# A hybrid encoder layer on one core: the first gate pair's accumulator moves to another PSUM pool, pooled parts to another SBUF pool, A21's preparation beside the last gate pair, and a fourth early gate tile

## The chip, the cores and the metric

The kernel runs on one core of a Trainium2 chip. The metric is device time in microseconds (us), the median of several runs; less is better. The engines are named as the profile names them: PE is TensorE's matmul, PEld its weight load, DVE is VectorE, ACT is ScalarE, POOL is GpSimd, and SP is the engine whose queue issues most of the loads.

## The reference, cut to what matters

One layer, 1024 tokens by 1024 channels, all in fp32:

```python
n = rmsnorm(h, norm_mix_pre[l])
proj = n @ w_in[l]
p_in = proj[..., :o0]                       # pooling branch, 4 groups, windows 2/4/8/16
qkv = proj[..., o0:o1]...                   # stick-breaking attention, 8 heads
xq = proj[..., o1:o2]...                    # cross attention into 256 memory tokens
gates = jax.nn.sigmoid(proj[..., o2:])...   # 3 branches x 1024 channels
y_pool = pool_mixer(p_in, w_pool_mix[l], pool_scale[l]) @ w_pool_o[l]
y_sb = stick_breaking_attention(q, k, v) @ w_sb_o[l]
y_x = memory_cross_attention(xq, mem_n, w_mem_kv[l]) @ w_x_o[l]
merged = gates[:, :, 0] * y_pool + gates[:, :, 1] * y_sb + gates[:, :, 2] * y_x
h = h + rmsnorm(merged @ w_out[l], norm_mix_post[l])
...                                         # then a SwiGLU layer of width 2816
```

The change is in the part from the projection `n @ w_in` to the start of stick-breaking attention.

## The kernel before, in words

**Precision by parts.** Every fp32 operand is split into a high and a low part (`parts`: ACT casts the high one, line 256, and DVE subtracts it to get the low one, line 257). `mm3` then runs three matmuls for each block (lines 170 to 172: high by high, high by low, low by high), mostly 128x128 weights against 128x512 columns.

**The projection by quarters.** The normed, transposed activations are cut into two column halves `c` (0, 1) and two depth halves: "A11", "A12" belong to `c` = 0 and "A21", "A22" to `c` = 1. A *pair* of 128-row output tiles is made by seven products rather than eight (a Strassen-like scheme), from the combinations S1 to S4 of the A quarters and matching combinations of the weight quarters b11 to b22 (function `pairs`). In a pair, `opening` makes product 11 in a bank X and product 12 in a bank Y; S2, S3 and 22 then go onto X, and S1 and S4 use another bank Y. The sums are taken on DVE: line 447 in the opening, line 471 after S4, line 476 after S3. Line 476 reads X, so product 22, which goes onto X, waits for it. xq, q, k, v and the gates of branch 0, output tiles 0 to 5 (`PAIRED`), are made in this way. The value product `v` is written out by hand, with two banks in X and two in Y (lines 774 to 805), and `to_values` splits its results on ACT (line 361) and DVE (line 362) into `d` tiles that POOL writes to DRAM (line 768).

**Plain gate tiles.** The other gate tiles go by plain products (`gate_step`: 12 matmuls for a depth half, 24 for a tile and a column half). `early` makes some of them, for `c` = 0 alone, while DVE still prepares S1 to S4, and `EARLY` says how many. The rest stand in the list `later`; `fill` takes from it in equal shares between the units of stick-breaking attention. A21 is needed by plain gate tiles with `c` = 1 alone.

**Work beside the pairs.** Memory attention (`recall`) and the pooling branch (`pooled`) are in a list `background`, one step of which `aside` starts at three points of each pair. A step of `pooled` loads raw projections, sums them on DVE (lines 663 to 681), splits the mixture into parts `mh` and `ml`, runs three matmuls into bank `pv`, and splits the result again (lines 687, 688) into `d` tiles that POOL writes to DRAM (line 692).

**What sets the order.** Tiles come from pools with fixed numbers of buffers: PSUM `pa` 3 banks, `pz` 2, `pt` 2, `pv` 1; SBUF `d` 6, `r` 4, `b2` 8, `ws` 3. A tile waits until an earlier tile in its buffer has been read for the last time. A scheduler reorders instructions between engines when the program is built, so the order on each engine is not that of the code; loads on the SP queue keep the code's order.

Of the kernel before, what the change touches and what calls it, by code (L numbers as in the profile page):

```python
# [9 lines left out]
F32R = mybir.dt.float32r  # L10
# [17 lines left out]
SCALE = 0.125  # L28
LEAD = 8
HOLD = 3  # L30
EARLY = 3
PAIRED = 6
FILL_FIRST = 4
FILL_LAST = 8
# [5 lines left out]
def hybrid_block(  # L40
# [47 lines left out]
    def t_act():  # L88
        return act.tile([P, C], F32R, tag="act", name="act")
# [7 lines left out]
    def t_b2(dt=F32):  # L97
        return b2p.tile([P, C], dt, tag="b2", name="b2")
# [4 lines left out]
    def t_d(dt=F32):  # L103
        return dp.tile([P, C + 16], dt, tag="d", name="d")
# [4 lines left out]
    def t_r(dt=F32):  # L109
        return rp.tile([P, C + 16], dt, tag="r", name="r")  # L110
# [7 lines left out]
    def ps_a():  # L118
        return pa.tile([P, C], F32, tag="pa", name="pa")

    def ps_z():
        return pz.tile([P, C], F32, tag="pz", name="pz")
# [132 lines left out]
    def parts(src, hi, lo, eng=nc.vector):  # L255
        nc.scalar.copy(hi, src)  # L256
        eng.tensor_sub(lo, src, hi.bitcast(F32))  # L257
        return hi, lo

    def normed_x(k, c, t, kept=False):  # L260
        if not kept:
            load(t, x[k, c])
        nc.vector.scalar_tensor_tensor(t, t, gain(G_PRE, k), rbc[c], ALU.mult, ALU.mult)
        return t
# [168 lines left out]
    def quarters(src, m):  # L433

        raw = [[None, None], [None, None]]
        for h, i in ((0, 0), (1, 0), (0, 1), (1, 1)):
            raw[h][i] = t_b2()
            load(raw[h][i], src[m + i, h])
        return raw

    def opening(raw, sink, other=ps_a):
        (b11, b12), (b21, b22) = raw
        X, Y = ps_a(), other()
        product(X, w_parts(b11), "11", True)
        p1 = copied(X)
        product(Y, w_parts(b21), "12", True)
        nc.vector.tensor_add(p1, Y, p1)
        sink(0, 0, p1)
        return X

    def pairs(jobs, raws=None):

        raws = raws or [jobs[0][0]()]
        ahead = len(raws)

        opened = [opening(raws[j], jobs[j][1], (ps_a, ps_z)[j]) for j in range(ahead)]
        for j, (_, sink) in enumerate(jobs):
            (b11, b12), (b21, b22) = raws[j]
            if len(raws) == j + 1 < len(jobs):
                raws.append(jobs[j + 1][0]())  # L460
            X, Y = opened[j], ps_a()
            t = b11
            nc.vector.tensor_sub(t, b12, t)
            product(Y, w_parts(t), "S1", True)
            s5 = copied(Y)
            aside()
            nc.vector.tensor_sub(t, b22, t)
            product(X, w_parts(t), "S2")
            s2 = copied(X)
            product(Y, w_parts(b22), "S4")  # L470
            nc.vector.tensor_add(s2, Y, s2)
            sink(0, 1, s2)
            aside()
            nc.vector.tensor_sub(b12, b22, b12)
            product(X, w_parts(b12), "S3")
            nc.vector.tensor_add(s5, X, s5)
            sink(1, 1, s5)
            nc.vector.tensor_sub(b21, b21, t)
            if len(opened) == j + 1 < len(jobs):
                opened.append(opening(raws[j + 1], jobs[j + 1][1]))  # L480
            product(X, w_parts(b21), "22")
            sink(1, 0, X)
            aside()
# [7 lines left out]
    def to_gate(b, m):  # L491
        def sink(c, i, t):
            u = t_g() if c == 1 and i == 0 else t
            nc.scalar.activation(u, t, AF.Sigmoid)
            nc.gpsimd.dma_start(gated[b][m + i][c], u)
        return sink
# [20 lines left out]
    def early(m):  # L517
        for half in range(2):
            w = w_parts(first_gate[half]) if m == 0 else split(w_gate[KT + m, half])
            gate_step(KT + m, half, 0, w)  # L520
# [10 lines left out]
    early(1)  # L531
    xq_raws.append(quarters(w_q, 0))
    early(2)
    for q in range(HK):
        nc.vector.tensor_sub(sums[q], sums[q], xs[q])
        A["S2"][q] = parts(sums[q], t_a(F32R), t_a(F32R))
# [116 lines left out]
    def pooled(g, c):  # L653
        def step():
            win = 2 << g
            p_in = t_c()
            load(p_in[:, :C], raw_d[g][c])
            if c == 1:
                nc.vector.memset(p_in[:, C:], 0.0)
            else:  # L660
                load(p_in[:, C:], raw_d[g][1][:, :16])
                nc.vector.tensor_mul(p_in[:, C:], p_in[:, C:], rbc[1][:, :16])
            nc.vector.tensor_mul(p_in[:, :C], p_in[:, :C], rbc[c])
            s = p_in
            step_, width = 1, C + 16
            while step_ < win:
                width -= step_
                nxt = t_c()
                nc.vector.tensor_add(nxt[:, :width], s[:, :width], s[:, step_ : step_ + width])
                s = nxt  # L670
                step_ *= 2
            e = slice(C - win + 1, C)
            if c == 1:
                fix = small.tile([P, 16], F32, tag="fix", name="fix")
                nc.vector.tensor_mul(fix[:, : win - 1], s[:, e], rcnt[:, 17 - win :])
            mixed = s[:, :C]
            nc.vector.scalar_tensor_tensor(
                mixed, mixed, 1.0 / win, p_in[:, :C], ALU.mult, ALU.subtract
            )
            if c == 1:  # L680
                nc.vector.tensor_sub(mixed[:, e], fix[:, : win - 1], p_in[:, e])
            mh, ml = parts(mixed, t_d(F32R)[:, :C], t_d(F32R)[:, :C])
            pm = ps_v()
            gs = slice(g * P, (g + 1) * P)
            mm3(pm, mix_h[:, gs], mix_l[:, gs], mh, ml, True, True)
            hi, lo = t_d(F32R)[:, :C], t_d(F32R)[:, :C]
            nc.scalar.activation(hi, pm, AF.Copy, scale=gain(G_POOL, g))
            nc.vector.scalar_tensor_tensor(
                lo, pm, gain(G_POOL, g), hi.bitcast(F32), ALU.mult, ALU.subtract
            )  # L690
            for t, d in zip((hi, lo), ph_d[g][c]):
                nc.gpsimd.dma_start(d, t)
        return step
# [78 lines left out]
            nc.vector.tensor_sub(dst[j], x_[j], y_[j])  # L772

    (b11, b12), (b21, b22) = raw
    X, Y = [ps_a(), ps_a()], [ps_a(), ps_z()]
    v_product(Y, two(b21), "12", True)
    p2 = [copied(t) for t in Y]
    aside()
# [25 lines left out]
    v_product(X, two(b21), "22")  # L804
    to_values(1, 0, X)

    pairs([(lambda m=m: quarters(w_gate, m), to_gate(0, m)) for m in range(0, PAIRED, 2)])
    while background:
        aside()
    for q in range(HK):  # L810
        u = normed_x(q, 1, t_d()[:, :C])
        A["21"][q] = parts(u, t_act(), t_act())

# [6 lines left out]
        for half in range(2)  # L822
        for c in range(1 if b == 1 and m < EARLY else 0, NC)
    ]
    gate_units = list(dict.fromkeys((t, half) for t, half, _ in later))
    gate_w = {}

# [575 lines left out]
```

## Time and profile before

| | |
|---|---|
| median of 3 runs | 1493.74 us (1491.47 to 1495.3) |
| the profiled execution's own time | 1493.64 us |
| its span, first to last instruction | 1491.9 us |
| PE busy | 1445.1 us (97%) |
| DVE busy | 1030.6 us (69%) |
| ACT busy | 702.3 us (47%) |
| POOL busy | 332.5 us (22%) |

The span is what the trace covers; the execution's own time lies 1.74 us above it. Busy shares are averages over the whole span; what a stage waits for is read from the stage.

### The profile page before, as it was taken

What the parts mean: (1) busy time and instruction counts of PE and PEld (TensorE: products, weight loads), DVE (VectorE), ACT (ScalarE), POOL (GpSimd) and SP (SyncE); (2) the same over time, 40 slices, a digit from 0 to 9 for tenths busy, and PEclk for the clock granted to TensorE, in tenths of its full rate; (3) what the DMA queues carried; (4) which work ended last, traced back from release to release, by engine and by line L of the source; (5) the groups of instructions that cost most, each with busy time, mean ns of one, the idle gap of its engine ahead of it and who ended that gap; (6) DMA issues with size and microseconds to landing.
All of it is one profiled execution on the core that took longest, in us unless ns stands there. A gap on an engine that the chain in (4) does not pass through costs nothing.

```text
span 1491.9 us, 20986 instructions
## 1 busy us (share of the span) xinstructions
PE 1445.1 (97%) x6926; PEld 1199.2 (80%) x6926; DVE 1030.6 (69%) x1718; ACT 702.3 (47%) x1399; POOL 332.5 (22%) x612
## 2 busy tenths in 40 slices
PE   9989999889999899999999999999999999999997
PEld 7867889668888788878887777888888887788876
DVE  8897878785886878655514597765566666579476
ACT  8555655444654666521235673223333333444453
POOL 0211121222322433444445310000011111000011
PEclk9999999999999999999999999999999999999999
DMA  7734455565432441575455454444455555664445
GB/s 240 233 100 131 145 170 171 184 217 185 125 96 95 151 128 64 170 248 167 152 162 195 144 181 147 152 133 128 136 192 195 192 195 199 227 190 155 112 129 197
DMA packets 125070, 243.68 MB, mean 163 GB/s; under 512 B 16528, under 2 KB 20128, under 8 KB 124960
## 3 DMA queue, kind: packets, MB, share of 16 engines
q1 hardware_dynamic: 96800, 171.00, 37.3%
q0 software_dynamic: 27584, 70.29, 13.5%
q8 instruction: 54, 0.88, 0.3%
q10 hardware_dynamic: 576, 1.05, 0.2%
q14 instruction: 56, 0.46, 0.1%
HBM read 172.01 MB, written 69.73 MB: 162 GB/s over the span
## 4 chain that ended last, share of the span: by engine, by line
PE 81%; issue 7%; DVE 6%; DMA 2%; ACT 2%; POOL 2%; SPq 0%; POOLq 0%; DVEq 0%; ACTq 0%
PE pa L170 15%; PE pa L172 15%; PE pa L171 15%; PE pz L172 5%; PE pz L170 5%; PE pz L171 5%; PE pt L172 3%; PE pt L170 3%; PE pt L171 3%; PE pt L895 2%; PE pv L170 1%; PE pv L910 1%; PE pv L171 1%; PE pv L907 1%; PE pv L172 1%
## 5 line engine op out<-in xcount | busy, mean ns | idle before, releaser
L170 PE MATMUL pa<-act,wh 128*128 128x512 f32 (+1 forms) x584 | 230.8, 395 | 8.8 <-DVE d L362 3.5
L172 PE MATMUL pa<-act,wl 128*128 128x512 f32 (+1 forms) x584 | 228.5, 393 | 2.9 <-DVE wl L257 2.6
L171 PE MATMUL pa<-act,wh 128*128 128x512 f32 (+1 forms) x584 | 229.4, 393 | 0.0
L256 ACT CAST wh<-b 128x512 fp32r<-128x512 f32 x152 | 93.5, 621 | 151.3 <-PE pa L171 91.0
L170 PEld LDWEIGHTS pa<-act,wh 128*128 128x128 f32 x584 | 110.9, 190 | 33.0 <-issue 4.2
L172 PEld LDWEIGHTS pa<-act,wl 128*128 128x128 f32 x584 | 110.7, 189 | 26.1 <-DVE wl L257 3.8
L171 PEld LDWEIGHTS pa<-act,wh 128*128 128x128 f32 x584 | 110.9, 190 | 21.1 <-issue 0.2
L257 DVE TENSOR_TENSOR wl<-b,wh 128x512 fp32r<-128x512 f32 x152 | 103.6, 686 | 29.8 <-ACT wh L256 25.1
L164 ACT CAST wh<-ws 128x512 fp32r<-128x512 f32 (+1 forms) x119 | 72.7, 611 | 102.6 <-PE pa L171 34.2
L256 ACT CAST wh<-ws 128x512 fp32r<-128x512 f32 x80 | 49.9, 625 | 105.1 <-DVE ws L1167 39.9
L165 POOL TENSOR_TENSOR wl<-ws,wh 128x512 fp32r<-128x512 f32 x52 | 69.1, 1337 | 71.9 <-ACT wh L164 71.9
L256 ACT CAST d<-b 128x512 fp32r<-128x512 f32 x66 | 40.8, 622 | 91.6 <-PE pt L171 47.2
L257 DVE TENSOR_TENSOR d<-b,d 128x512 fp32r<-128x512 f32 x66 | 45.4, 691 | 52.4 <-ACT d L256 49.0
L170 PE MATMUL pa<-a,wh 128*128 128x512 f32 x192 | 75.9, 398 | 5.7 <-ACT wh L256 3.5
L165 DVE TENSOR_TENSOR wl<-ws,wh 128x512 fp32r<-128x512 f32 (+1 forms) x67 | 44.8, 673 | 48.9 <-ACT wh L164 29.7
L171 PE MATMUL pa<-b,wh 128*128 128x512 f32 x192 | 75.6, 395 | 0.0
L172 PE MATMUL pa<-a,wl 128*128 128x512 f32 x192 | 74.6, 392 | 0.0
L176 DVE TENSOR_TENSOR d<-pt,d 128x512 fp32r<-128x512 f32 (+1 forms) x96 | 60.7, 637 | 17.4 <-ACT d L175 16.9
L1133 POOL DMA_DIRECT2D ff<-c x44 | 23.7, 540 | 214.9 <-DVE c L1188 123.6
L175 ACT CAST d<-pt 128x512 fp32r<-128x512 f32 (+1 forms) x96 | 53.0, 559 | 37.3 <-PE pt L895 26.4
L876 DVE TENSOR_TENSOR_SCAN r<-a,zero 128x512 f32<-128x512 f32 (+1 forms) x64 | 54.4, 852 | 18.1 <-POOL a L864 18.0
L257 DVE TENSOR_TENSOR wl<-ws,wh 128x512 fp32r<-128x512 f32 x80 | 54.9, 689 | 16.6 <-ACT wh L256 14.2
(429 smaller groups left out, 3982.0 us busy)
## 6 DMA issues: line engine op xcount, KB each, us to landing
b<-in_w_ffn_in_dram SPq DMA_DIRECT2D x88, 256.0 KB, 2.7
d<-gt SPq DMA_DIRECT2D x48, 256.0 KB, 3.0
ws<-in_w_ffn_in_dram SPq DMA_DIRECT2D x44, 256.0 KB, 2.7
ff<-c POOLq DMA_DIRECT2D x44, 256.0 KB, 2.9
b<-ffS SPq DMA_DIRECT2D x44, 256.0 KB, 2.7
ws<-in_w_gate_dram SPq DMA_DIRECT2D x40, 256.0 KB, 3.8
gt<-g POOLq DMA_DIRECT2D x39, 256.0 KB, 3.0
b<-ff SPq DMA_DIRECT2D x33, 256.0 KB, 3.8
```

Source lines behind the costliest of these rows:

```text
L164: nc.scalar.copy(wh[:, :n], ws[:, :n])
L165: lo.tensor_sub(wl[:, :n], ws[:, :n], wh[:, :n].bitcast(F32))
L170: nc.tensor.matmul(ps, lh, rh, start=first, stop=False, skip_group_check=onto)
L171: nc.tensor.matmul(ps, lh, rl, start=False, stop=False, skip_group_check=onto)
L172: nc.tensor.matmul(ps, ll, rh, start=False, stop=last, skip_group_check=onto)
L175: nc.scalar.copy(hi, ps)
L176: nc.vector.tensor_sub(lo, ps, hi.bitcast(F32))
L256: nc.scalar.copy(hi, src)
L257: eng.tensor_sub(lo, src, hi.bitcast(F32))
L876: nc.vector.tensor_tensor_scan(ex[:, lo + 1 : C + 1], rest[:, lo:], zero.broadcast_to([P, C - lo]), start, ALU.mult, ALU.add,)
L895: nc.tensor.transpose(ptr[:, col + n * P : col + (n + 1) * P], att[i, j // 4][:, (j % 4) * P : (j % 4 + 1) * P], ident,)
L1133: nc.gpsimd.dma_start(ff_d[n][k], t)
```

## The change

`EARLY` goes from 3 to 4, with one more call of `early`. `pairs` takes a bank function for the first job's X (`first`), and the gate pairs pass `ps_z`; in the value product the two banks of Y are taken ahead of those of X. `pooled` takes `mh` and `ml` from pool `r` in place of `d`. A21's loads and normalization are called by `beside_last` at the start of the last gate pair, into `b2` tiles in place of `d` tiles, and its parts follow the pairs directly. The first four entries of `later` are sorted so that both depth halves of a tile with `c` = 0 come ahead of those with `c` = 1.

```diff
-EARLY = 3
+EARLY = 4
...
-    def opening(raw, sink, other=ps_a):
+    def opening(raw, sink, other=ps_a, bank=ps_a):
         (b11, b12), (b21, b22) = raw
-        X, Y = ps_a(), other()
+        X, Y = bank(), other()
...
-    def pairs(jobs, raws=None):
+    def pairs(jobs, raws=None, beside_last=None, first=ps_a):
...
-        opened = [opening(raws[j], jobs[j][1], (ps_a, ps_z)[j]) for j in range(ahead)]
+        opened = [
+            opening(raws[j], jobs[j][1], (ps_a, ps_z)[j], (first, ps_a)[j]) for j in range(ahead)
+        ]
...
-            if len(raws) == j + 1 < len(jobs):
+            if len(raws) == j + 1 and j + 1 < len(jobs):
                 raws.append(jobs[j + 1][0]())
+            elif beside_last is not None:
+                beside_last()
...
     early(2)
+    early(3)
...
-            mh, ml = parts(mixed, t_d(F32R)[:, :C], t_d(F32R)[:, :C])
+            mh, ml = parts(mixed, t_r(F32R)[:, :C], t_r(F32R)[:, :C])
...
-    X, Y = [ps_a(), ps_a()], [ps_a(), ps_z()]
+    Y, X = [ps_a(), ps_z()], [ps_a(), ps_a()]
...
-    pairs([(lambda m=m: quarters(w_gate, m), to_gate(0, m)) for m in range(0, PAIRED, 2)])
+    a21 = []
+    pairs(
+        [(lambda m=m: quarters(w_gate, m), to_gate(0, m)) for m in range(0, PAIRED, 2)],
+        beside_last=lambda: a21.extend(normed_x(q, 1, t_b2()) for q in range(HK)),
+        first=ps_z,
+    )
+    for q in range(HK):
+        A["21"][q] = parts(a21[q], t_act(), t_act())
     while background:
         aside()
-    for q in range(HK):
-        u = normed_x(q, 1, t_d()[:, :C])
-        A["21"][q] = parts(u, t_act(), t_act())
...
+    later[:2 * NC] = sorted(later[: 2 * NC], key=lambda n: (n[2], n[1]))
```

Three places of the built order show what moves. The change's line numbers are those of the changed file (a line such as 540 there is line 535 before).

The first is DVE while S2 to S4 are prepared, from the second depth half of the third early tile on (`wl_1101`; `wl` made at line 165 is the low part of a loaded weight tile). Before:

```order
L165 TENSOR_TENSOR wl_1101<-ws_1098,wh_1100 128x512
L535 TENSOR_TENSOR r_1012<-r_1012,act_230 128x512
L165 TENSOR_TENSOR wl_1262<-ws_1259,wh_1261 128x512
L257 TENSOR_TENSOR wl_1284<-b2_1023,wh_1283 128x512
L539 TENSOR_TENSOR act_292<-act_292,d_990 128x512
L257 TENSOR_TENSOR act_1180<-d_982,act_1179 128x512
L257 TENSOR_TENSOR wl_1302<-b2_1025,wh_1301 128x512
```

After:

```order
L165 TENSOR_TENSOR wl_1101<-ws_1098,wh_1100 128x512
L540 TENSOR_TENSOR r_1012<-r_1012,act_230 128x512
L165 TENSOR_TENSOR wl_1122<-ws_1119,wh_1121 128x512
L544 TENSOR_TENSOR act_292<-act_292,d_990 128x512
L257 TENSOR_TENSOR act_1220<-d_982,act_1219 128x512
L547 TENSOR_TENSOR d_979<-d_982,d_979 128x512
L257 TENSOR_TENSOR a_1166<-d_990,a_1165 128x512
L165 TENSOR_TENSOR wl_1141<-ws_1138,wh_1140 128x512
```

Two more weight splits (`wl_1122`, `wl_1141`, the fourth early tile) stand there, and the first pairs' own splits come later; the subtraction at line 467 that product S2 of the first pair waits for has two more DVE instructions ahead of it than before.

The second is PE at the end of the value product, where the first gate pair begins (`pa_3193` is its X and `pa_3194` its Y before; `pv_3101` is a step of `pooled`). Before:

```order
L171 MATMUL pa_3193<-a_1136,wh_3287 128x512
L172 MATMUL pa_3193<-a_1135,wl_3288 128x512
L170 MATMUL pv_3101<-d_3097,wh_1261 128x512
L171 MATMUL pv_3101<-d_3098,wh_1261 128x512
L172 MATMUL pv_3101<-d_3097,wl_1262 128x512
L170 MATMUL pa_3194<-act_613,wh_3213 128x512
L171 MATMUL pa_3194<-act_614,wh_3213 128x512
```

After (`pz_3233` is X and `pa_3234` Y, `pa_3280` the bank of product S1):

```order
L172 MATMUL pa_3234<-act_628,wl_3254 128x512
L170 MATMUL pv_3141<-r_3137,wh_1301 128x512
L171 MATMUL pv_3141<-r_3138,wh_1301 128x512
L172 MATMUL pv_3141<-r_3137,wl_1302 128x512
L170 MATMUL pz_3233<-a_1160,wh_3327 128x512
L171 MATMUL pz_3233<-a_1161,wh_3327 128x512
L172 MATMUL pz_3233<-a_1160,wl_3328 128x512
```

Before, product 12 (`pa_3194`) stands behind S2 and both steps of `pooled`; after, products 11 and 12 are done first, and S2 follows. The 12 matmuls of S2 are followed by S1 in `pa_3280`.

The third is DVE at the end of the last gate pair (`c_3739` and `c_3702` are the pair's sums before, `c_3791` and `c_3754` after; line 263 normalizes A21, and `act` tiles from line 257 are its low parts). Before:

```order
L471 TENSOR_TENSOR c_3739<-pa_3684,c_3739 128x512
L476 TENSOR_TENSOR c_3702<-pa_3598,c_3702 128x512
L263 SCALAR_TENSOR_TENSOR d_3800<-d_3800,g_sb_99,r_513 128x512
L263 SCALAR_TENSOR_TENSOR d_3807<-d_3807,g_sb_99,r_513 128x512
L263 SCALAR_TENSOR_TENSOR d_3814<-d_3814,g_sb_99,r_513 128x512
L257 TENSOR_TENSOR act_3804<-d_3800,act_3803 128x512
```

After:

```order
L263 SCALAR_TENSOR_TENSOR b2_3733<-b2_3733,g_sb_99,r_513 128x512
L257 TENSOR_TENSOR act_3857<-b2_3727,act_3856 128x512
L693 SCALAR_TENSOR_TENSOR d_3612<-pv_3607,g_sb_99,d_3611 128x512
L674 TENSOR_TENSOR c_3707<-c_3703 128x513
L257 TENSOR_TENSOR act_3861<-b2_3730,act_3860 128x512
L257 TENSOR_TENSOR act_3865<-b2_3733,act_3864 128x512
L682 SCALAR_TENSOR_TENSOR c_3707<-c_3707,c_3696 128x512
L257 TENSOR_TENSOR r_3711<-c_3707,r_3710 128x512
L475 TENSOR_TENSOR c_3791<-pa_3736,c_3791 128x512
L693 SCALAR_TENSOR_TENSOR d_3719<-pv_3714,g_sb_99,d_3718 128x512
L480 TENSOR_TENSOR c_3754<-pa_3638,c_3754 128x512
```

A21's eight DVE instructions moved from behind the last pair's two sums to ahead of them.

## Rows read from the trace of the kernel before

**Rows 1.** The page's first part: busy time, share of the span, instructions.

```profile
PE 1445.1 (97%) x6926; PEld 1199.2 (80%) x6926; DVE 1030.6 (69%) x1718; ACT 702.3 (47%) x1399; POOL 332.5 (22%) x612
```

**Rows 2.** Timeline of PE, 95 to 113 us: start, duration, line, operands, [idle before <-releaser].

```profile
98.11 0.50 PE L172 MATMUL pa<-act,wl 128*128 128x512 f32 x1 [1.01 <-DVE wl L257]
...
104.18 0.79 PE L170 MATMUL pa<-a,wh 128*128 128x512 f32 x1 [3.50 <-ACT wh L256]
...
112.54 0.36 PE L591 MATMUL pz<-c,r 128*128 128x256 f32 x1 [1.34 <-DMA r<-xq]
```

**Rows 3.** Windows: stretch, length, busy by engine (instructions), granted clock, DMA share, GB/s.

```profile
104.10:107.20 3.10, 3.02 (x8) 2.40 (x9) 2.99 (x5) 1.58 (x4) 0.53 (x1) 0.53 0.62 172
268.90:274.20 5.30, 5.30 (x13) 4.14 (x14) 0.85 (x2) 0.72 (x3) 1.59 (x3) 0.50 1.05 339
335.50:339.30 3.80, 3.80 (x12) 2.97 (x11) 2.24 (x4) 1.40 (x3) 0.00 (x0) 0.55 0.68 189
250.20:329.70 79.50, 71.50 (x317) 57.00 (x315) 62.46 (x115) 37.96 (x70) 21.33 (x40) 0.96 0.62 190
317.80:329.70 11.90, 9.97 (x42) 7.34 (x40) 7.34 (x14) 4.10 (x7) 2.67 (x5) 1.00 0.89 269
345.00:645.00 300.00, 293.56 (x1610) 249.62 (x1608) 224.26 (x343) 170.87 (x379) 102.84 (x266) 1.00 0.40 128
680.00:720.00 40.00, 40.00 (x175) 32.65 (x174) 21.07 (x28) 8.29 (x14) 17.85 (x14) 1.00 0.50 157
```

**Rows 4.** Timeline of DVE, 80 to 103 us.

```profile
80.51 0.69 DVE L165 TENSOR_TENSOR wl<-ws,wh 128x512 fp32r<-128x512 f32 x1
81.11 0.69 DVE L535 TENSOR_TENSOR r<-r,act 128x512 f32<-128x512 f32 x1
...
102.78 0.69 DVE L467 TENSOR_TENSOR b<-b,b 128x512 f32<-128x512 f32 x1
```

**Rows 5.** Timeline of PE, 263 to 275 us.

```profile
263.70 0.51 PE L170 MATMUL pv<-d,wh 128*128 128x512 f32 x1 [1.00 <-ACT d L256]
264.60 0.50 PE L171 MATMUL pv<-d,wh 128*128 128x512 f32 x1 [0.40 <-DVE d L257]
...
268.87 0.77 PE L170 MATMUL pa<-act,wh 128*128 128x512 f32 x1 [3.53 <-DVE d L362]
```

**Rows 6.** Timeline of ACT, 263 to 271 us.

```profile
266.06 0.69 ACT L687 ACTIVATE d<-pv,g_sb 128x512 fp32r<-128x512 f32 x1 [2.42 <-DMA v<-d]
```

**Rows 7.** Timeline of PE, 320 to 335 us.

```profile
320.54 0.50 PE L171 MATMUL pv<-d,wh 128*128 128x512 f32 x1 [0.75 <-DVE d L257]
...
325.96 0.50 PE L170 MATMUL pa<-b,wh 128*128 128x512 f32 x1 [0.44 <-ACT c L424]
...
329.75 0.50 PE L170 MATMUL pa<-act,wh 128*128 128x512 f32 x1 [0.78 <-DVE c L476]
...
334.77 0.50 PE L170 MATMUL pa<-act,wh 128*128 128x512 f32 x1 [1.97 <-ACT wh L256]
```

**Rows 8.** Timeline of DVE, 325 to 333 us.

```profile
325.47 0.75 DVE L688 SCALAR_TENSOR_TENSOR d<-pv,g_sb,d 128x512 fp32r<-128x512 f32 x1 [2.09 <-ACT d L687]
...
329.00 0.69 DVE L476 TENSOR_TENSOR c<-pa,c 128x512 f32<-128x512 f32 x1 [2.18 <-PE pa L172]
329.61 2.07 DVE L263 SCALAR_TENSOR_TENSOR d<-d,g_sb,r 128x512 f32<-128x512 f32 x3
331.59 1.29 DVE L257 TENSOR_TENSOR act<-d,act 128x512 fp32r<-128x512 f32 x2
```

**Rows 9.** Timeline of the SP queue's loads, 324 to 337 us.

```profile
324.50 3.11 SPq L116 DMA_DIRECT2D d<-in_x_dram  x4
327.67 9.33 SPq L116 DMA_DIRECT2D ws<-in_w_gate_dram  x5
```

**Rows 10.** Waits of PE, 345 to 640 us: us in total, times, longest.

```profile
PE pv L907 <- DVE b L376: 2.0, 4, 1.0
PE pa L172 <- DVE wl L257: 1.6, 1, 1.6
```

## The prediction

> **What bounds the kernel now.** I read the page's busy shares first: PE is busy 97% of the span and DVE 69% [rows 1], so the time is PE's own work plus the places where PE stands still. The page's shares can't say where these are. The timeline of PE shows them: three short stretches hold the largest waits, one near 104 us, one near 269 us, one around 330 us [rows 2, 5, 7]. The windows show what a wait costs on top: behind each of them the granted clock is 0.53, 0.50 and 0.55 over a few us, which is the lower of its two levels (1.2 instead of 2.4 GHz), though PE has matmuls without a break there [rows 3]. The pace to compare with is that of an undisturbed stretch, 175 matmuls in 40.00 us, 0.229 us each [rows 3].
>
> **Step A, the fourth early tile.** Before, product S2 of the first pair waits 3.50 us for ACT's cast of its weights (104.18 us) [rows 2]. That cast waits for a DVE subtraction, line 467, which starts at 102.78 us; DVE instructions of this size follow each other every 0.60 us there (80.51 to 81.11 us) [rows 4]. The fourth tile adds 24 matmuls on PE, 24 x 0.229 = 5.5 us, ahead of S2, taken from the later fill. It adds two weight loads, two casts and two subtractions. The loads and casts are hidden: ACT is busy 1.58 of 3.10 us in that stretch [rows 3]. The two subtractions stand ahead of line 467 and DVE has no gap, so S2 can start 2 x 0.60 = 1.2 us later than before. PE thus does 5.5 us of work for a delay of 1.2: 4.3 us. The slow clock behind the wait goes too, as the wait left is about the size of the one at 98.11 us (1.01 us), behind which the clock did not fall: 3.10 us for 8 matmuls against 1.83 gives 1.3 us. Of the 5.6 us I take 5.2, since line 447's sums, ahead of line 467 on DVE, now wait for a PE that comes later. Bounds: 3.9 (the clock falls anyway, and those tenths are lost) to 6.9 (also the DMA wait of 1.34 us at 112.54 us [rows 2] goes, because the first memory scores stand 14 matmuls later).
>
> **Step B, the banks.** At 268.87 us product 12 of the first gate pair waits 3.53 us for a `pa` bank that the value product's last splits (line 362) still read, and just before it two waits of 1.00 and 0.40 us are for the parts of a `pooled` step [rows 5]. Why the splits are late stands on ACT: line 687 waits 2.42 us until a value tile in its `d` buffer has been written to DRAM [rows 6]; line 361 is queued behind it, and DVE's 362 waits for that. The change acts on both ends: X lies in `pz` and Y in a bank read earlier, so products 11 and 12 need no splits; and with `mh` and `ml` out of pool `d`, each `pooled` step takes two of the six `d` buffers in place of four. Waits of 4.93 us, and 13 matmuls in 5.30 us that should take 2.97 (2.3 us), are at stake: 7.3 us. What is late next is S1, whose bank is now the one that the splits hold. By the order PE does 37 matmuls between the value product and that wait, in place of 28, 2.1 us more cover; with ACT's 2.42 us gone as well, 4.5 us against the wait of 3.53 and the 1.40 that no longer delay PE leave about 0.4; I put 1.0. Step B is worth 6.3 us, between 2.1 (the splits come no earlier) and 7.3.
>
> **Step C, A21 beside the last pair.** Around 330 us PE waits 0.75, 0.44, 0.78 and 1.97 us [rows 7], and 12 matmuls in 3.80 us should take 2.7 (1.1 us) [rows 3]: 5.0 us. The 1.97 is for the cast of a later gate tile's weights. Their loads stand behind A21's four loads in the SP queue, which went out at 324.50 us, and went out at 327.67 us [rows 9]. A21's loads now go into `b2` tiles that the second pair has left, ahead of the heads' q and k loads; these tiles are free well before, so I put the four loads (3.11 us of the queue) at nothing; if they were late, the first heads would be late by up to that. The price is on DVE: four normalizations (three in 2.07 us) and four subtractions (two in 1.29) [rows 8], 5.3 us, now ahead of the sums at lines 471 and 476, for which product 22 waits. From 317.8 to 329.7 us DVE is busy 7.34 us [rows 3]; with 5.3 more that is 12.7, while PE without its 0.75 and 0.44 us needs 10.7. So line 476 comes 2.0 us late where it was 0.78. Step C: 5.0 - 2.0 = 3.0 us, between -1.4 (all 5.3 on the path, and the slow clock again, 1.1) and 5.0.
> What the rows show is that DVE idles 2.09 and 2.18 us just there, waiting for others [rows 8], which takes in most of A21. The Trainium skill (PSUM — Partial Sum Buffer, "Engine vs sequencer instructions") says that VectorE's queue is strict first in, first out, which speaks against this move: whatever stands ahead of a sum delays it, needed or not. By that rule without the idle time, step C would be 5.0 - 5.3 = -0.3 us and the sum 1483.5 us.
>
> **Step D, given back.** From 345 to 645 us PE is busy 293.56 of 300 us [rows 3], so the 5.5 us taken from its fill come off the time, unless they covered a wait. The largest groups of waits there are 2.0 and 1.6 us [rows 10]. I give back a fifth, 1.1 us; bounds 5.5 back, and 3.6 gained if both groups go, since the shares of `fill` come out more even. Sorting `later` costs nothing: the same matmuls with the same weights.
>
> **The sum.** 5.2 + 6.3 + 3.0 - 1.1 = 13.4 us off the profiled execution's 1493.64 (span 1491.9 plus 1.74): **1480.2 us**. The median of the runs shown is 0.1 above that execution.
>
> **The rivals.**
> DVE takes the place of the banks. From 250.2 to 329.7 us DVE is busy 62.46 us; with A21 67.8. PE's 71.50 there hold 2.3 us of slow clock, so it needs 69.2 [rows 3]: DVE would have to be busy 98% of a stage without PE's waits. For it: that number. Against it: the loads it adds come at the end, where DVE idles. Step C falls to -1.4: 1484.6 us. Chance 0.17.
> The change doesn't do what it says at the bank: the value tiles' writes, not the pooled parts, hold the `d` buffers (line 687's releaser is a value tile), and the wait moves from product 12 to S1. Step B is 2.1: 1484.4 us. Chance 0.11.
> The fill was cover, so its 5.5 us are given back: 1484.6 us. For it: PE waits in the attention stage at all; against it: under 2.2% of that stretch. Chance 0.07.
> Slower: attention starves. The units with the shortest work get one half tile each, and if the waits in each of the four head pairs grow to what rows 10's groups hold now in all, and half as much again, 5.4 us, then 4 x 5.4 = 21.6 us come back: 1493.64 - 14.5 + 21.6 = 1500.7 us. It decides from 14.5 us of new waits on (19 for over 0.3%). Nothing in the profile asks for it. Chance 0.03.
>
> **How the numbers follow.** The forecast has 0.62, with a range of its own from 1476 to 1484. A measurement of this kernel can tell about 0.3%, 4.5 us, from no change. The upper end goes to two of the first three rivals together (13.4 - 4.4 - 4.2 = 4.8 us gained, 1488.8); the lower end takes in two thirds of what the upper bounds add (1.7 + 1.0 + 2.0 + 4.7 = 9.4 us). That gives 1473.5 to 1488.5. Faster: the forecast and the single rivals, but for 0.09 where two or three of them meet: 0.88; same 0.09; slower 0.03.
>
> **What the changed profile would show.** A: no wait over 1.5 us on PE before S2 of the first pair, and a clock of 1.0 around it. B: product 12 of the first gate pair without a wait, S1 with one under 1.5 us, no slow clock near 265 us; a wait of over 3 us at S1 would be the second rival. C: the gate weights' casts no longer waited for; a wait of some 2 us at line 476 (480 of the changed file) or at the casts queued behind line 471 on ACT; over 4 us there is the first rival. D: PE's waits in the attention stage within 2 us of before's. The prediction fails if a new wait of over 3 us with a slow clock behind it shows up elsewhere, since that alone costs over 5 us.

## The result, and the profile after

The changed kernel takes 1479.87 us (median), the kernel before on the same chip 1492.61 us; the ratio of their runs is 0.9904, 95% interval 0.9888 to 0.9919, so it is about 1% faster. The forecast was 1480.2 us. The profiled execution took 1478.91 us, 14.73 less than the one of before, with a span of 1477.2 us. One run of 4814.21 us is left out of the comparison.

The time is right, but its terms are not: steps A and B gained more than was forecast, step C gained nothing, and step D gave back more. The rest of the document is about that.

The page's first part, which answers to [rows 1]:

```profile
PE 1441.9 (98%) x6926; PEld 1198.7 (81%) x6926; DVE 1029.8 (70%) x1720; ACT 702.9 (48%) x1401; POOL 332.2 (22%) x612
```

PE does as many matmuls as before. The place to read is where it doesn't run. Three stages cover the change: up to the first matmul of the value product; from there through the three gate pairs, to 15 us after the last matmul of product S3; and the attention stage with the merge of the branches, up to the transposes of line 1068 (1078 of the changed file). First the windows of these three stages before, then the same after:

```profile
0.00:209.60 209.60, 197.86 (x979) 164.97 (x979) 168.82 (x344) 128.52 (x265) 38.02 (x87) 0.99 0.55 173
209.60:343.40 133.80, 123.49 (x691) 106.08 (x692) 104.69 (x199) 65.98 (x129) 26.85 (x52) 0.96 0.60 185
343.40:813.50 470.10, 462.35 (x2347) 387.86 (x2346) 301.62 (x449) 220.41 (x477) 192.16 (x342) 1.00 0.46 146
```

```profile
0.00:207.20 207.20, 202.46 (x1003) 169.44 (x1003) 169.85 (x346) 130.24 (x268) 38.56 (x88) 1.00 0.56 178
207.20:334.80 127.60, 122.91 (x712) 107.07 (x713) 103.11 (x199) 66.73 (x132) 27.37 (x53) 1.00 0.68 206
334.80:799.00 464.20, 455.13 (x2303) 381.99 (x2302) 301.44 (x449) 218.28 (x475) 190.76 (x340) 0.99 0.45 144
```

Length less PE's busy time: 11.7, 10.3 and 7.8 us before, 4.7, 4.7 and 9.1 after. The clock went up from 0.99 and 0.96 to 1.00 in the first two stages, and down to 0.99 in the third. The first two stages got better, the third worse.

Now place by place. PE's timeline from 95 to 114 us holds three waits, where [rows 2] had 1.01, 3.50 and 1.34 us (start, duration, line, operands, idle before and its releaser, as in all timelines here):

```profile
102.22 0.50 PE L172 MATMUL pa<-act,wl 128*128 128x512 f32 x1 [0.78 <-DVE wl L257]
...
105.28 0.50 PE L170 MATMUL pa<-a,wh 128*128 128x512 f32 x1 [0.47 <-ACT wh L256]
...
106.28 0.50 PE L170 MATMUL pa<-a,wh 128*128 128x512 f32 x1 [0.27 <-ACT wh L256]
```

S2 of the first pair starts at 105.28 us, 1.10 later than before, with 24 more matmuls done. The second place is the first gate pair. From 257 to 275 us, where [rows 5] had 1.00, 0.40 and 3.53, PE waits nowhere; the windows say it with 18.00 of 18.00 us. The ACT instruction of [rows 6] (line 692 now) waits 0.29 us for PE and for no transfer:

```profile
95.00:108.00 13.00, 11.48 (x48) 8.53 (x47) 13.00 (x22) 5.72 (x10) 2.13 (x4) 1.00 0.29 83
257.00:275.00 18.00, 18.00 (x81) 14.88 (x80) 14.83 (x31) 11.31 (x22) 5.86 (x11) 1.00 0.82 253
```

```profile
260.25 0.69 ACT L692 ACTIVATE d<-pv,g_sb 128x512 fp32r<-128x512 f32 x1 [0.29 <-PE pv L172]
```

The third is the last gate pair. PE's timeline from 295 to 335 us; the waits of [rows 7] are gone and others stand there:

```profile
302.66 0.50 PE L170 MATMUL pa<-act,wh 128*128 128x512 f32 x1 [1.03 <-ACT g L498]
...
311.75 0.50 PE L170 MATMUL pa<-a,wh 128*128 128x512 f32 x1 [2.34 <-ACT c L424]
...
316.20 0.50 PE L170 MATMUL pv<-r,wh 128*128 128x512 f32 x1 [1.00 <-ACT r L256]
```

The 2.34 us is for the copy (line 424) out of S1's bank, into which S4 goes next. ACT's timeline just there shows what the copy stood behind:

```profile
306.84 0.62 ACT L256 CAST act<-b 128x512 fp32r<-128x512 f32 x1 [0.17 <-DVE b L263]
309.32 0.62 ACT L256 CAST act<-b 128x512 fp32r<-128x512 f32 x1 [1.85 <-DVE b L263]
309.85 0.68 ACT L692 ACTIVATE d<-pv,g_sb 128x512 fp32r<-128x512 f32 x1
310.59 0.62 ACT L256 CAST act<-b 128x512 fp32r<-128x512 f32 x1
311.11 0.58 ACT L424 COPY c<-pa 128x512 f32<-128x512 f32 x1
```

The casts `act<-b` make A21's high parts. One of them waits 1.85 us for DVE's normalization, and the copy is queued behind it. The gate weights' loads now go out at 310.62 us on the SP queue (327.67 in [rows 9]) and nothing waits for them.

The fourth is the attention stage. PE's waits there, where [rows 10] had 2.0 and 1.6 us as the largest groups:

```profile
PE pv L917 <- DVE b L376: 3.0, 3, 1.2
PE pv L917 <- DVE d L176: 2.0, 2, 1.8
```

The longest, 1.85 us at 378.15 us, has the slow clock behind it, and so have the waits around 630 us, where the branches are merged:

```profile
378.00:386.00 8.00, 7.84 (x36) 6.93 (x37) 8.00 (x12) 5.18 (x11) 4.01 (x11) 0.79 0.34 118
629.00:640.00 11.00, 9.74 (x34) 7.52 (x35) 5.30 (x8) 3.69 (x6) 8.21 (x7) 0.84 0.96 326
```

### The profile page after: what moved, and what is told of

The parts are those of the page before. It is cut to its first block, busy times and chain, and to the rows that moved or that the text cites. A ratio compares the mean times of both kernels' runs of the same rounds, so it can differ in the third digit from the quotient of the medians.

```text
span 1477.2 us, 20998 instructions
## 1 busy us (share of the span) xinstructions
PE 1441.9 (98%) x6926; PEld 1198.7 (81%) x6926; DVE 1029.8 (70%) x1720; ACT 702.9 (48%) x1401; POOL 332.2 (22%) x612
## 4 chain that ended last, share of the span: by engine, by line
PE 89%; DVE 5%; ACT 2%; issue 2%; DMA 1%; POOL 0%; SPq 0%; DVEq 0%; POOLq 0%; ACTq 0%
PE pa L170 17%; PE pa L172 17%; PE pa L171 17%; PE pz L172 6%; PE pz L170 6%; PE pz L171 6%; PE pt L172 3%; PE pt L170 3%; PE pt L171 3%; PE pt L905 2%; PE pv L917 1%; PE pv L920 1%; PE pz L868 1%; PE pv L170 1%; PE pv L171 1%
## 5 line engine op out<-in xcount | busy, mean ns | idle before, releaser
L170 PE MATMUL pa<-act,wh 128*128 128x512 f32 (+1 forms) x576 | 225.4, 391 | 2.3 <-ACT wh L256 1.0
L172 PE MATMUL pa<-act,wl 128*128 128x512 f32 (+1 forms) x576 | 223.7, 390 | 1.7 <-DVE wl L257 1.2
L171 PE MATMUL pa<-act,wh 128*128 128x512 f32 (+1 forms) x576 | 224.4, 390 | 0.0
L170 PEld LDWEIGHTS pa<-act,wh 128*128 128x128 f32 x576 | 108.4, 188 | 24.5 <-ACT wh L256 1.9
L171 PEld LDWEIGHTS pa<-act,wh 128*128 128x128 f32 x576 | 108.4, 188 | 20.6 <-issue 0.2
L176 DVE TENSOR_TENSOR d<-pt,d 128x512 fp32r<-128x512 f32 (+1 forms) x96 | 60.3, 637 | 15.8 <-ACT d L175 15.1
L181 POOL TENSOR_TENSOR rc<-rv,mhalf 128x1 f32<-128x1 f32 (+2 forms) x15 | 14.7, 980 | 230.3 <-DVE rv L1306 198.6
```

Of the source, the lines that this page charges most:

```text
L170: nc.tensor.matmul(ps, lh, rh, start=first, stop=False, skip_group_check=onto)
L171: nc.tensor.matmul(ps, lh, rl, start=False, stop=False, skip_group_check=onto)
L172: nc.tensor.matmul(ps, ll, rh, start=False, stop=last, skip_group_check=onto)
L176: nc.vector.tensor_sub(lo, ps, hi.bitcast(F32))
```

## One account for all kernels

For each kernel below, the loss of a stage is the sum of PE's waits that the timeline lists in it and of the time lost to the lower clock (length times one less the granted clock, in windows of 5 us). For the kernel before and the change:

```
               to the value product   value product, gates   attention, merge
before         11.69 + 1.70 = 13.39   10.30 + 5.15 = 15.45   7.58 + 0.00 =  7.58
change          4.74 + 0.00 =  4.74    4.37 + 0.00 =  4.37   8.86 + 3.40 = 12.26
difference                   - 8.65                - 11.08               + 4.68
forecast        A            - 5.2     B and C     - 9.3     D           + 1.1
```

The three differences sum to -15.1 us, and the spans differ by 14.7. The account counts the lower clock also where PE stands still and loses nothing by it, 1.0 us in all for the kernel before. It is of one profiled execution for each kernel, and these don't all stand for the median: that of a21_later is the longest of its six (1486.31 us against a median of 1480.77), that of no_a21_last6 the longest of its four (1481.77 against 1477.25), those of low_on_pool and last6 the shortest (1478.8 against 1481.59, 1475.11 against 1476.97). What the account leaves over up to the transposes, which should be one number, lies between 773 and 778 us. So differences of 5 us or less between two kernels can't be rested on it alone; the single places can.

All twelve experiments, with the ratio to the kernel before on the same chip (its median was 1492.6 us beside the change and 1493.7 to 1495.4 beside the experiments); "early" is the number of early tiles, "A21" whether its preparation stands beside the last pair (moved) or behind it:

```
                early A21     ratio   95% interval      losses by stage
change           4    moved   0.9904  0.9888 - 0.9919    4.74   4.37  12.26
early_only       4    as was  0.9992  0.9981 - 1.0002    6.47  18.33  13.51   banks, r as before
no_early         3    moved   0.9884  0.9866 - 0.9903   14.52   5.98   4.30
no_bank          4    moved   0.9937  0.9919 - 0.9956    5.94  10.71   9.83
no_r             4    moved   0.9946  0.9931 - 0.9962    7.27  13.21   8.64
bank_r_only      3    as was  0.9933  0.9920 - 0.9946   13.56   4.39   8.17
no_a21           4    as was  0.9863  0.9844 - 0.9882    4.96   6.82   5.45
low_on_pool      4    moved   0.9917  0.9901 - 0.9934    4.59   7.58   8.56
casts_behind     4    moved   0.9913  0.9896 - 0.9930    5.80   3.99  12.38
a21_later        4    later   0.9918  0.9903 - 0.9934    6.38   7.16  16.41
no_sort          4    moved   0.9915  0.9899 - 0.9930    4.44   5.29  13.42
last6            4    moved   0.9892  0.9878 - 0.9906    4.85   5.47  11.54
no_a21_last6     4    as was  0.9890  0.9873 - 0.9906    6.97  11.37  10.54
```

## The experiments

**The early tile: early_only and no_early.** The kernel before with the fourth tile alone, and the change without it.

```diff
-EARLY = 3
+EARLY = 4
...
     early(2)
+    early(3)
```

> The kernel before with the fourth early gate tile and nothing else. Theory (the tile fills PE's 3.50 us wait before product S2 of the first pair, and what it takes from the later fill comes off the time): 5 to 8 us faster than before, no wait over 1 us before S2, the clock at 1.0 there. Rival (the fill was cover in the attention stage): within 2 us of before, with some 5 us of new waits between 345 and 640 us.

> The change without the fourth early tile. Theory (the parts add up): 6 to 8 us faster than before, that is 5 to 8 us slower than the change, with the 3.5 us wait and the slow clock near 104 us back. Rival (the early tile gives nothing that lasts): as fast as the change, 13 to 15 us faster than before.

Both rivals have the time right: alone the tile is worth nothing (1494.43 us, 0.9992), and the change without it is no slower (1479.75 us, 0.9884). Yet at its own place it does what was forecast, and more: the first stage loses 13.4 to 14.5 us in the three kernels with three tiles (before among them) and 4.4 to 7.3 us in the eleven with four. In early_only 6.9 us are gained there, and 2.9 and 5.9 are lost again in the two stages behind.

**The banks and the r tiles: no_bank, no_r and bank_r_only.** The change without `first=ps_z` and with X and Y in the order of before; the change with the pooled parts in `d` tiles; and the kernel before with these two edits and nothing else.

```diff
-    Y, X = [ps_a(), ps_z()], [ps_a(), ps_a()]
+    X, Y = [ps_a(), ps_a()], [ps_a(), ps_z()]
...
-        first=ps_z,
```

```diff
-            mh, ml = parts(mixed, t_r(F32R)[:, :C], t_r(F32R)[:, :C])
+            mh, ml = parts(mixed, t_d(F32R)[:, :C], t_d(F32R)[:, :C])
```

> The change with the first gate pair's X in pool pa again and the value product's banks in the old order. Theory (both the bank and the d buffers made the 3.5 us wait): product 12 of the first gate pair waits again, 1 to 3.5 us; 3 to 7 us slower than the change. Rival (freeing d buffers alone is enough): within 1 us of the change, no such wait.

> The change with the pooled parts in pool d again. Theory (the value product's last splits are late because d buffers are short): the wait moves to product S1 of the first gate pair, 1 to 4 us, 2 to 6 us slower than the change. Rival (the bank alone is enough): no wait at S1, within 1 us of the change.

> The kernel before with step B alone: X of the first gate pair in a pz bank, the value product's banks swapped, the pooled parts in r tiles. Theory 1, the parts add: the early tile is worth nothing, A21 beside the last pair costs 6 us, so step B alone must be worth nearly 20 us, about 1474. Theory 2, the parts do not add, and what A21's move costs is lost in the attention stage, whose order the scheduler makes anew for each kernel: step B alone is worth what the trace shows at its own places, the 4.93 us of waits and the slow clock behind them in the first gate pair, and the wait of 0.75 us in the last, some 8 us, less or more by what the attention stage happens to lose: 1482 to 1489, with the early stage's waits (1.01, 3.50, 1.34 us) still there and product 12 and S1 of the first gate pair without a wait.

Without the bank (1486.26 us) product 12 of the first gate pair waits for the value splits again, in PE's timeline from 255 to 275 us, with the clock at 0.77 behind it:

```profile
263.96 0.77 PE L170 MATMUL pa<-act,wh 128*128 128x512 f32 x1 [2.50 <-DVE d L362]
```

```profile
263.90:271.00 7.10, 7.04 (x24) 5.75 (x25) 3.27 (x6) 3.29 (x5) 1.60 (x3) 0.77 0.79 256
```

That is 4.2 of the 6.3 us that its second stage loses more than the change's. Most of the rest is in the last pair, where the wait for line 424 is 2.95 us and the slow clock stands behind it.

Without the r tiles (1487.54 us) the wait moves to S1, as the second rival had it, and a larger one appears in the last pair, for a cast of pooled parts:

```profile
272.62 0.47 PE L170 MATMUL pa<-act,wh 128*128 128x512 f32 x1 [1.99 <-DVE d L362]
...
317.68 0.49 PE L170 MATMUL pv<-d,wh 128*128 128x512 f32 x1 [4.87 <-ACT d L256]
```

At the first of these places ACT's line 361 waits 2.78 us until a value tile has been written to DRAM:

```profile
271.64 0.37 ACT L361 CAST d<-pa 128x256 fp32r<-128x256 f32 x1 [2.78 <-DMA v<-d]
```

At the second, DVE makes the last piece of the mixture (line 686) at 316.77 us, and the cast starts 0.07 us after its end. In this kernel's order A21's four normalizations and three of its subtractions stand ahead of that piece on DVE, from 309.21 us on, and DVE has no gap there. So this wait points to DVE's queue; that a `d` buffer is missing is not shown:

```profile
316.77 0.17 DVE L686 TENSOR_TENSOR c<-fix,c 128x15 f32<-128x15 f32 x1
317.01 0.62 ACT L256 CAST d<-c 128x512 fp32r<-128x512 f32 x1 [2.45 <-issue]
```

So at the first gate pair it takes both: the bank takes the splits off PE's path, and the r tiles let them run. Both by themselves (1483.57 us, 0.9933) give 10 us, and the trace of bank_r_only puts all of it into the second stage (15.45 to 4.39 us). Its first stage loses as much as before, and the third differs by 0.6. The theory that the parts simply add asked for 1474 and falls; the other, 1482 to 1489, holds.

**A21: no_a21, low_on_pool, casts_behind and a21_later.** A21 made behind the pairs again; its subtractions on POOL; its casts kept behind the pair's copies on ACT; and A21 made still later, behind two half tiles of `later`.

```diff
-        beside_last=lambda: a21.extend(normed_x(q, 1, t_b2()) for q in range(HK)),
...
-    for q in range(HK):
-        A["21"][q] = parts(a21[q], t_act(), t_act())
     while background:
         aside()
+    for q in range(HK):
+        u = normed_x(q, 1, t_d()[:, :C])
+        A["21"][q] = parts(u, t_act(), t_act())
```

```diff
-        A["21"][q] = parts(a21[q], t_act(), t_act())
+        A["21"][q] = parts(a21[q], t_act(), t_act(), nc.gpsimd)
```

```diff
-        nc.scalar.copy(t, ps)
+        tc.keep_in_program_order(nc.scalar.copy(t, ps))
...
-        A["21"][q] = parts(a21[q], t_act(), t_act())
+        hi, lo = t_act(), t_act()
+        tc.keep_in_program_order(nc.scalar.copy(hi, a21[q]))
+        nc.vector.tensor_sub(lo, a21[q], hi.bitcast(F32))
+        A["21"][q] = hi, lo
```

a21_later takes both A21 blocks of the first of these diffs out and puts the one with `t_d` here:

```diff
-    fill(FILL_FIRST)
+    fill(2)
+    for q in range(HK):
+        u = normed_x(q, 1, t_d()[:, :C])
+        A["21"][q] = parts(u, t_act(), t_act())
+    fill(FILL_FIRST - 2)
```

> The change with A21 made behind the gate pairs in d tiles again, loads included. Theory (A21 beside the last pair removes about as much as it brings: 1.97 us and a slow clock against waits of 2.34 and 1.00 us near 312 and 316 us): within 2 us of the change; the wait of 2.34 us gone, one of 1 to 2 us for a gate weight's cast back. Rival (the move is worth the 3.0 us of the forecast or more): 3 us or more slower than the change.

> The change with A21's four low parts subtracted on POOL instead of DVE. Theory (the 2.34 us wait near 312 us is ACT's queue: the copy of S1's result stands behind casts of A21 that wait for DVE's normalizations, and DVE is full there): two subtractions fewer ahead of the third normalization bring the copy 1.2 us earlier, so the wait falls to 1.0 to 1.4 us, and the time by 1 to 2 us. Rival (the copy is late by its own place): the wait stays at 2.3 us, the time as the change's.

> The change with A21's four casts kept behind the last pair's two bank copies on ACT. Theory (as above, ACT's queue order makes the wait): the 2.34 us wait is gone, the time falls by 1.5 to 3 us unless the first use of A21's parts then waits. Rival (PE waits for DVE in any order, since DVE is full): a wait of the same size, 2 us or more, moves to the last pair's sums, the time stays.

> The change with A21 made behind the first two half tiles of later, so that its loads stand behind those of the gate weights and its DVE work behind the last pair's sums. Without beside_last (A21 directly behind the pairs), DVE took A21's normalizations ahead of the sum that product 22 waits for, and stood 1.98 us for A21's load from DRAM, with that sum queued behind it: 3.61 us of PE's wait and 1.65 us of slow clock. Theory 1: the queue is the cause; with the sum ahead, that wait is at most 0.8 us (as in the kernel before) and the clock stays, some 4 us less than that kernel's 0.9863: about 1468 to 1470. Theory 2: A21 is then late for the first gate tile with c = 1, and PE waits there for ACT's casts or DVE's subtractions, 3 us or more, with the slow clock: 1472 to 1476.

no_a21 has the lowest time of all: 1472.59 us, 0.9863, faster than the change (the intervals don't meet), which neither its theory nor its rival had. At the place itself it is not better. Its PE timeline near 320 us has one wait of 3.61 us with the slow clock behind it, and DVE's shows why:

```profile
320.61 0.79 PE L170 MATMUL pa<-act,wh 128*128 128x512 f32 x1 [3.61 <-DVE c L480]
```

```profile
316.81 1.43 DVE L263 SCALAR_TENSOR_TENSOR d<-d,g_sb,r 128x512 f32<-128x512 f32 x2 [1.98 <-DMA d<-in_x_dram]
318.60 0.75 DVE L263 SCALAR_TENSOR_TENSOR d<-d,g_sb,r 128x512 f32<-128x512 f32 x1 [0.36 <-DMA d<-in_x_dram]
319.27 0.69 DVE L257 TENSOR_TENSOR act<-d,act 128x512 fp32r<-128x512 f32 x1
319.87 0.68 DVE L480 TENSOR_TENSOR c<-pa,c 128x512 f32<-128x512 f32 x1
```

The sum at line 480, for which product 22 waits, could run when PE ends S3 near 317 us. It runs at 319.87 us, because A21's normalizations stand ahead of it and wait for their own load. The Trainium skill (PSUM — Partial Sum Buffer, "Engine vs sequencer instructions") calls the queues of ScalarE and VectorE strict first in, first out; the trace agrees, on DVE here and on ACT with the 1.85 us of the change. In the prediction this rule was set against DVE's idle time and taken for covered; both traces show PE waiting behind such a queue, 2.34 us with A21 beside the pair and 3.61 behind it. By that rule without the idle time the prediction had put step C at -0.3 us, which comes nearer to what its stage shows than the 3.0 us that it took.

casts_behind takes A21's casts from ahead of the copy. The wait for the copy falls from 2.34 to 1.25 us, so the casts cost 1.09 of it, and two small waits (0.49 and 0.79 us) come up behind it. What is left stands behind a split of `pooled` (line 692), which itself waits for PE; the copy follows it at 310.71 us:

```profile
310.12 0.69 ACT L692 ACTIVATE d<-pv,g_sb 128x512 fp32r<-128x512 f32 x1 [2.77 <-PE pv L172]
```

The time stays (1480.54 us), where the theory asked for 1.5 to 3 us less. low_on_pool leaves the wait for the copy (2.16 us, where its theory asked for 1.4 at most), and a subtraction takes 1.3 to 1.7 us on POOL; 1481.59 us. a21_later, with the sum ahead of A21 on DVE, has no wait for line 480 any more, so the queue was the cause of the 3.61 us; but A21 is now late itself, as the second theory had it (the wait is shorter than its 3 us). Its PE timeline, in the first gate tile with `c` = 1:

```profile
331.44 0.50 PE L171 MATMUL pa<-act,wh 128*128 128x512 f32 x1 [2.02 <-DVE act L257]
```

Its second stage is no better than that of no_a21 (7.16 against 6.82 us). The kernel takes 1480.77 us, above the ranges of both theories (1468 to 1476); in its profiled execution, 5.5 us longer than that, the third stage loses 16.41 us against 5.45.

**What the attention stage loses: no_sort, last6 and no_a21_last6.** The change without the sorting of `later`; with two more half tiles (a depth half of a plain gate tile each) in the attention stage (54, as before the change, in place of 52); and no_a21 with these two.

```diff
-    later[:2 * NC] = sorted(later[: 2 * NC], key=lambda n: (n[2], n[1]))
```

```diff
-FILL_LAST = 8
+FILL_LAST = 6
```

> The change without the sorting of the first four later entries. Theory (sorting costs and brings nothing): within 1.5 us of the change. Rival (it hides A21's parts): a new wait of 1 us or more for A21's parts behind the last gate pair, 2 us or more slower.

> The change with FILL_LAST 6 in place of 8, so that 54 half tiles stand in the attention stage, as before the change, and not 52; 6 are left for the end. Theory 1, the fill was cover: with the two back the attention and the stage behind it lose about what they lost before (7.6 us of waits and slow clock) in place of 13.5, so about 1474. Theory 2, the amount says nothing and the waits come from the order that the scheduler makes: the waits are at other places than in the change and their sum can go either way, 1475 to 1484; in that case a kernel with 54 can lose as much as the change does.

> The change with A21 made behind the pairs as before (the fastest kernel so far, 0.9863) and 54 half tiles in the attention stage in place of 52. Theory 1, the attention stage's loss follows the order that the scheduler builds and nothing that the edit does: the order of TensorE's instructions there differs from that of each kernel run so far, so the waits stand at new places and their sum with the slow clock lies anywhere between 4.3 and 16.4 us, the ends seen so far (5.45 us without the two half tiles): 1471 to 1483. Theory 2, more fill covers more: 5.45 us or less, 1472 or less. In both the stages ahead of the attention lose what they lose without the two half tiles, about 12 us.

Sorting is worth nothing that can be measured (1481.07 us). last6 is 1476.97 us with an interval that meets the change's, and its third stage still loses 11.54 us (the 13.5 us that its expectation gives the change are 12.26 in the account). no_a21_last6 is 1477.25 us where no_a21 without the two half tiles is 1472.59; the intervals just overlap. In its profiled execution, 4.5 us longer than its median, the third stage lost more (10.54 against 5.45), and so did the two ahead (18.3 us, where 12 were expected). So the amount of fill alone doesn't set the loss: with 52 half tiles the stage lost 5.45 to 16.41 us, with 54 it lost 4.30 to 11.54.

What the waits follow is the order that the scheduler builds. Compared by source line and tile names, PE's instructions in this stage stand in the same order in the change and in no_bank, and differ in 2 places between low_on_pool and no_r, while the change and low_on_pool differ in more than 50. And the waits go with it. First the change, then no_bank, which is some 7 us later by then:

```profile
378.15 0.39 PE L917 MATMUL pv<-d,a 128*128 128x256 f32 x1 [1.85 <-DVE d L176]
...
538.52 0.39 PE L917 MATMUL pv<-d,a 128*128 128x256 f32 x1 [1.23 <-DVE b L376]
...
545.18 0.39 PE L917 MATMUL pv<-d,a 128*128 128x256 f32 x1 [1.17 <-DVE b L376]
```

```profile
385.14 0.39 PE L916 MATMUL pv<-d,a 128*128 128x256 f32 x1 [1.85 <-DVE d L176]
...
545.38 0.38 PE L916 MATMUL pv<-d,a 128*128 128x256 f32 x1 [1.23 <-DVE b L376]
...
552.05 0.38 PE L916 MATMUL pv<-d,a 128*128 128x256 f32 x1 [1.16 <-DVE b L376]
```

Then low_on_pool and no_r:

```profile
379.00 0.50 PE L867 MATMUL pz<-c 128*128 128x512 f32 x1 [1.13 <-ACT b L871]
...
384.38 0.51 PE L172 MATMUL pa<-act,wl 128*128 128x512 f32 x1 [0.76 <-DVE wl L257]
...
549.59 0.50 PE L172 MATMUL pa<-act,wl 128*128 128x512 f32 x1 [0.91 <-DVE wl L257]
```

```profile
385.73 0.50 PE L867 MATMUL pz<-c 128*128 128x512 f32 x1 [1.11 <-ACT b L871]
...
391.11 0.50 PE L172 MATMUL pa<-act,wl 128*128 128x512 f32 x1 [0.74 <-DVE wl L257]
...
555.97 0.50 PE L172 MATMUL pa<-act,wl 128*128 128x512 f32 x1 [0.91 <-DVE wl L257]
```

Kernels that share an order share these waits to 0.02 us, whatever edit made them; kernels with another order have others. The losses of the stage go the same way: 8.56 and 8.64 us in low_on_pool and no_r, 7.58 and 8.17 in the kernel before and bank_r_only, whose orders differ in some 15 places, and 9.83 to 13.42 in the change, no_bank, no_sort and casts_behind, the last two within some 20 places of the change. (Not all repeat so well: the wait for line 164's cast where the branches are merged is 1.28 us in the change and 0.74 in no_bank.) The loss also takes in whether the clock falls: behind the 1.85 us it fell in both, behind the waits of the merge in the change alone, which makes most of the difference between their 12.26 and 9.83 us. What in an order makes a wait long was not followed further.

One thing speaks for a share of the early tile in it: the three kernels with three early tiles have 4.30, 7.58 and 8.17 us, and of the eleven with four only no_a21 lies below 8. As the kernel before and bank_r_only share most of their order, these are two orders, too few to tell that from chance.

## Why the prediction was right, point by point

**Step A, the early tile: right at its place, under-sized.** No wait over 1.5 us before S2, clock 1.00, S2 1.10 us later (1.2 forecast). The stage gained 8.65 us, not 5.2, and more than the upper bound of 6.9 (6.92 in early_only, the tile by itself): S2's waits fell by 2.76 us and the clock's 1.70 are gone, much as forecast, but so are the transfer's 1.34 us, which stood only in the upper bound, and three that were not in the sum: 0.77 us for line 447 at 96.40 us, 0.92 of a wait of 1.56 for line 597 at 142.73 us, and a start-up wait of 0.98 us at 7.24 us that the early tile doesn't touch.

**Step B, the banks: right, under-sized.** Product 12 without a wait, S1 too, clock 1.00. bank_r_only gives 10 us by its ratio and 11.1 by its second stage, where 6.3 was forecast and 7.3 the upper bound. S1's wait, put at 1.0, is not there; and two items that the prediction gave to step C come with B: the 0.75 us of the pooled parts in the last pair, and the slow clock behind the wait of 1.97. That wait itself stays in bank_r_only (2.09 us), but the clock doesn't fall behind it; no run ties this to the banks.

**Step C, A21: the step that failed at its own place.** The casts of the gate weights are no longer waited for, as forecast, and a wait of some 2 us came for work queued behind A21, as forecast, though on ACT and for S4 and not on DVE for line 476. The term of 3.0 us isn't there. From bank_r_only to no_early the waits of 0.48, 0.79 and 2.09 us went, and 2.34 us and 1.70 of slow clock came; the second stage loses 5.98 against 4.39 us. With four early tiles it loses 4.37 against 6.82. Around nothing, then, with either sign: the term set DVE's and PE's busy time against each other and left out that what is queued first is waited for, on ACT and DVE.

**Step D, what comes back: mis-sized.** 1.1 us were forecast, 4.7 came back. Its own test held, since the waits of attention and merge are 8.86 us against 7.58, within 2 us. What wasn't counted is the slow clock behind two of them, 3.40 us. The reason that the prediction gave, less fill to cover waits, is not the one that the runs show: the fill's amount alone doesn't set the loss, and the waits go with the newly built order. For a forecast this is a term with a spread of 4 to 16 us and no sign to be read from the diff, and one fifth of the fill was no basis for it.

**The sum.** A and B gave 5.2 + 6.3 = 11.5 us in the forecast and about 20 in the trace; C and D gave +1.9 in the forecast and about -5 in the trace. The errors offset each other, so it is luck that 1480.2 was so close. (A slip in the range: two thirds of 9.4 us below 1480.2 is 1473.9, not 1473.5.) The sign of failure, a new wait of over 3 us with a slow clock behind it, did not come: the largest new wait is 2.34 us, without one. Of the rivals, DVE in place of the banks did not come in its size: line 480 is not waited for in the change, though ACT's 1.85 us for DVE stand behind the wait of 2.34. Nor did the attention starve (4.7 us back, not 21.6). The second did not come either; its wait at S1 shows when the r tiles are undone. The third, the fill as cover, has step A's small net worth right (nothing in early_only), by a cause that the runs with two half tiles more don't bear out.

**What stays open.** The parts don't add. The fourth tile is worth 10.5 us on bank_r_only (0.9933 to 0.9863, with the sorting, which in the change gave nothing) and nothing on no_early (0.9884 to 0.9904, overlapping intervals); A21's move gains 7 us with three early tiles (0.9933 to 0.9884, the sorting again with it) and costs 6 with four (0.9863 to 0.9904). The third stage's losses have the sign of each of these differences, but the account isn't close enough to say that they make all of it.

## What to carry to other kernels

Where a scheduler builds the order, price an edit at its own place from the trace, and then give every later stage that is rebuilt a spread of its own, taken from the losses of kernels that differ only there; here it was as large as any term of the edit. Try the parts of a bundled change in pairs as well as alone: the kernel with the lowest time was the change less one of its parts, and the fourth tile, worth nothing alone (0.9992), would not have told it. A21's move alone was not run. And an instruction that waits for its own load must not stand in DVE's or ACT's queue ahead of one that PE needs, even on an engine that has idle time.

## What the runs showed of the hardware

Whether the clock falls behind a wait can't be told from the wait's length alone: it fell to 0.50 behind the 1.56 us at 142 us in bank_r_only and not behind the same 1.56 us before; behind the 2.34 us for line 424 in no_early and not in the change; and not behind 2.09 us in bank_r_only, where it did behind 1.97 us before. A fall cost 1.7 us in most places and 3.4 in others (behind the 3.53 us of before). A load from DRAM took longer in one kernel than in another at the same place: A21's four loads landed after 4.8 us (median) in no_a21 and 6.0 in no_a21_last6, where DVE waited 1.98 and 3.32 us for them and PE 3.61 and 4.52 us for line 480.
